# Rotary embedding and two pools' differences kept in their PSUM banks, in an encoder layer on one core

## The chip, the core and the metric

The kernel runs on one core of one Trainium2 chip. Five engines take part, each with its own in-order queue of instructions: TensorE (PE) multiplies matrices into the eight banks of PSUM, VectorE (DVE) and ScalarE (ACT) do element-wise work from and to SBUF and PSUM, GpSimd (POOL) does element-wise work in SBUF, and SyncE (SP) issues transfers. They wait for each other through semaphores. The metric is device time in microseconds, the median of three runs.

## What is computed

One layer of a bidirectional encoder, 512 tokens of width 1024: a half-step feed-forward block, a mixing block, another half-step feed-forward block and a final norm. The change touches the mixing block:

```python
u = rms_norm(h, mix_norm[l]) @ w_in[l]
q, k, v, pc = jnp.split(u, [512, 640, 768], axis=-1)
q = apply_partial_rope(q.reshape(B, S, 8, 64), cos, sin)     # first 16 of 64 dims
k = apply_partial_rope(k.reshape(B, S, 2, 64), cos, sin)
a = window_attention(q, k, v, sink_logits[l])                # 4 blocks of 128 tokens, +-128
# four groups of 128 channels, windows 2, 4, 8, 16:
p = ((mean_window(pc) - pc) @ pool_w) * pool_scale           # per group
h = h + concat([a, p]) @ w_out[l]
```

The rotation is `rot * cos + rot_half * sin`, where `rot_half` exchanges the two halves of the 16 rotated dimensions and negates one.

## The kernel before

Everything is kept transposed, channels on the 128 partitions and 512 tokens along the free dimension. Products are made to full precision out of three reduced-precision ones (`mm3`, L131 to L133): each operand is split into a high part, which ACT rounds (`wh`, `ah`, `pdh`, ...), and the rest, which DVE or POOL subtracts (`wl`, `al`, `pdl`, ...). Weights come in 1 MB transfers (`raw`) and are split half by half in `split_next` (L103, L104); a table says which halves of w_in and w_out POOL subtracts rather than DVE (`WIN_POOL`, `WOUT_POOL`, L30 and L32).

The mixing block (L356 on) runs so. PE projects keys and values, then pool group 3, query tile 0, pool group 2, query tiles 1, 2, 3, pool groups 1 and 0; each projection takes eight `mm3` and leaves its result in one PSUM bank. DVE rotates keys and queries in `rope` (L393): `stream_shuffle` from the bank into `rtmp`, bank times `cr` into `u`, `rtmp` times `sr` into `rtmp`, and the sum into `u`. ACT and DVE then split `u` into `kk`/`kl` (L419 to L421) or `qq` (L428, L429); two head halves of 64 partitions, a rounding by ACT and a subtraction by DVE for each. Values go through a transpose on PE and are split into `vv` and `vz` (L439 to L441); `vz` is a copy that DVE casts.

Each pool group starts in `pool_means` (L448): DVE scales the bank into `uu`; POOL widens the sums by doubling (`s`, L463), mends the edges (L469) and makes the sum `dd` (L472); DVE subtracts the token (`less_token`, L475); ACT and DVE split the difference into `pdh` and `pdl` (`halves`, L479, L480). These steps stand in lists (`later`) of which each step of the main flow takes one (`eased`), with `AFTER` empty steps ahead of the subtraction. `pool_linear` (L489) multiplies the difference by the group's matrix (the three matmuls ps<-pdh,pwh and so on), and first takes what is left of its list.

Attention goes by blocks of 128 tokens and two head groups of four: a score is two matmuls (L556, L557), a masked minimum on DVE (L558) and an exponential on ACT (L561); POOL scales the rows (L568); PE turns them (L585), ACT and DVE split them (`ph`, `pl`, L589, L590), and PE multiplies by the values (L600, L601). A plan (L656) weaves these with the last projections, the pool linears and the output projection. Ahead of the third and fourth score stand six fill matmuls each (L554). A scheduler places the instructions in each engine's queue and allots the banks; it may move an instruction forward or back among those of its engine, which the order below shows.

Of the kernel before, what the change touches and what calls it, by code (L numbers as in the profile page):

```python
# [8 lines left out]
F32 = mybir.dt.float32  # L9
F32R = mybir.dt.float32r  # L10
AF = mybir.ActivationFunctionType
ALU = mybir.AluOpType
# [3 lines left out]
S = 512  # L16
# [8 lines left out]
F0 = 3  # L25
WARM = 10
AFTER = 11
EARLY = 12
LAG = 4
WIN_POOL = (5,)  # L30
FIRST_SPARE = 7
WOUT_POOL = (0, 3, 6)  # L32
POOL_W = (2, 4, 8, 16)
PAD = 8

# [2 lines left out]
def encoder_layer(ctx: ExitStack, tc: tile.TileContext, xT, w1h, w1gu, w1d, win, wout, w2h, w2gu, w2d,  # L38
                  gains, gfin, sinks, poolw, pscale, cosT, sinT, edges, out):
    nc = tc.nc  # L40
# [112 lines left out]
    ps = bank()  # L153
# [202 lines left out]
    with tc.tile_pool(name="mix", bufs=1) as mp:  # L356
        cr = mp.tile([P, S], F32, name="cr")
        sr = mp.tile([P, S], F32, name="sr")
# [24 lines left out]
        vv = mp.tile([P, NT, 2, P], F32R, name="vv")  # L383
        vz = mp.tile([P, NT, 2, P], F32R, name="vz")
# [6 lines left out]
        swap = [i + 8 if i < 8 else i - 8 if i < 16 else i for i in range(32)]  # L391

        def rope(ps, rot):  # L393
            u = base.tile([P, S], F32, name="u", tag="u", bufs=2)
            nc.vector.stream_shuffle(rot, ps, swap)
            nc.vector.tensor_tensor(u, ps, cr, op=ALU.mult)
            nc.vector.tensor_tensor(rot, rot, sr, op=ALU.mult)
            nc.vector.tensor_tensor(u, u, rot, op=ALU.add)
            return u

        def project(box):

# [29 lines left out]
        def values():  # L432
            ps = bank()
            for b in range(NT):
                nc.tensor.transpose(ps[:, b * P:(b + 1) * P], vT[:, b * P:(b + 1) * P], ident)
            pv4 = ps.rearrange("p (b c) -> p b c", b=NT)
            for g in range(2):
                r, o = rows[g], rows[1 - g]
                nc.scalar.copy(vv[:, :, g, r], pv4[:, :, r])  # L439
                nc.vector.tensor_copy(vz[:, :, g, r], vv[:, :, g, r].bitcast(F32))  # L440
                nc.vector.tensor_tensor(vv[:, :, g, o], pv4[:, :, r], vv[:, :, g, r].bitcast(F32),  # L441
                                        op=ALU.subtract)

        pdh = mp.tile([P, 4, S], F32R, name="pdh")
        pdl = mp.tile([P, 4, S], F32R, name="pdl")
        later = []

        def pool_means(gi, ps):  # L448
            w = POOL_W[gi]
            half = w // 2  # L450
            e0 = 2 * (half - 1)
            uu = mp.tile([P, S + 128], F32, name="uu", tag="pl", bufs=3)[:, :S + 2 * PAD]
            n = S + 2 * PAD
            nc.gpsimd.memset(uu[:, :PAD], 0.0)
            nc.gpsimd.memset(uu[:, n - PAD:], 0.0)
            nc.vector.tensor_tensor(uu[:, PAD:PAD + S], ps, rstd, op=ALU.mult)
            box = {"cur": uu}

            def widen(step):
                m = n - 2 * step + 1  # L460
                cur = box["cur"]
                nxt = mp.tile([P, S + 128], F32, name="s1", tag="s1", bufs=2)
                nc.gpsimd.tensor_tensor(nxt[:, :m], cur[:, :m], cur[:, step:step + m], op=ALU.add)  # L463
                box["cur"] = nxt

            def scale():
                cur, o = box["cur"], PAD - half
                for a, e in ((o, e0), (o + S + 1 - half, e0 + half)):
                    nc.gpsimd.tensor_tensor(cur[:, a:a + half], cur[:, a:a + half], edge[:, e:e + half],  # L469
                                            op=ALU.mult)  # L470
                box["dd"] = mp.tile([P, S], F32, name="dd", tag="ph", bufs=3)
                nc.gpsimd.tensor_tensor(box["dd"], cur[:, o:o + S], cur[:, o + 1:o + 1 + S], op=ALU.add)  # L472

            def less_token():
                nc.vector.scalar_tensor_tensor(box["dd"], box["dd"], 0.5 / w, uu[:, PAD:PAD + S],  # L475
                                               op0=ALU.mult, op1=ALU.subtract)

            def halves():
                nc.scalar.copy(pdh[:, gi, :], box["dd"])  # L479
                nc.vector.tensor_tensor(pdl[:, gi, :], box["dd"], pdh[:, gi, :].bitcast(F32),  # L480
                                        op=ALU.subtract)

            wait = [lambda: None]
            steps = []
            while 1 << len(steps) < w:
                steps.append(lambda step=1 << len(steps): widen(step))
            later.append(steps + [scale] + (AFTER - len(steps)) * wait + [less_token, halves])

        def pool_linear(gi):  # L489
            while later[3 - gi]:  # L490
# [40 lines left out]
        last_pools = projected(1) + projected(0)  # L531
        weave([eased(f) for f in last_pools[:EARLY]], [])

# [208 lines left out]
def _arrange(inputs):  # L742
# [41 lines left out]
    rot = HD // 4  # L784
    inv = np.float32(500000.0) ** (-np.arange(0, rot, 2, dtype=np.float32) / np.float32(rot))
    ang = np.arange(S, dtype=np.float32)[None, :] * inv.astype(np.float32)[:, None]
    cosT = np.ones((P, S), np.float32)
    sinT = np.zeros((P, S), np.float32)
    for b in (0, HD):
        for j in range(rot // 2):  # L790
            cosT[b + j] = cosT[b + j + 8] = np.cos(ang[j])
            sinT[b + j] = -np.sin(ang[j])
            sinT[b + j + 8] = np.sin(ang[j])
    o["cosT"], o["sinT"] = cosT, sinT
    e = []
    for w in POOL_W:
# [28 lines left out]
```

## Time and profile before

| | us |
|---|---|
| median of 3 runs (lowest, highest) | 891.33 (891.25, 892.61) |
| the profiled execution | 892.52 |
| its span, first to last instruction | 890.7 |
| PE busy | 871.7 (98%) |
| DVE busy | 416.2 (47%) |
| ACT busy | 306.5 (34%) |
| POOL busy | 305.7 (34%) |
| mean granted clock of PE | 0.995 of full |

The shares are means over the whole span. The mixing block's first part, where projections end and attention starts, lies between about 385 and 465 us; the feed-forward blocks before and after it leave PE hardly any idle time. Matmul rows overlap, so PE counts as busy until the end of its last row, and a wait is printed in brackets behind the instruction that ended it, with the releasing engine, tile and line.

### The profile page before, as it was taken

The page shows a single profiled execution, that of the slowest core. Times are in us where ns is not written, and L with a number is a line of the kernel's source. Part 1 is how long each engine was busy: PE and PEld are TensorE (multiplying, and loading weights), DVE is VectorE, ACT ScalarE, POOL GpSimd, SP SyncE. Part 2 cuts the span into 40 slices and gives each one's busy share as a digit, 9 for nine tenths or more (in the row PEclk, how much of TensorE's full clock was granted, in tenths as well). Part 3 has the DMA queues.
Part 4 walks back from the last instruction along what each step waited for, and adds up shares of the span by engine and source line. Part 5 has one row for each costly group of instructions (what it writes and reads, how often), then busy time and mean ns, then how long its engine had stood idle before and what let it go on. Part 6 is the DMA issues. An engine that isn't in the chain of part 4 may idle for free.

```text
span 890.7 us, 9727 instructions
## 1 busy us (share of the span) xinstructions
PE 871.7 (98%) x3918; PEld 720.2 (81%) x3918; DVE 416.2 (47%) x519; ACT 306.5 (34%) x454; POOL 305.7 (34%) x252
## 2 busy tenths in 40 slices
PE   9999999999999999999689999999999999999996
PEld 7888888888888888888668888888888888888885
DVE  6454444444433322659788643444444444322235
ACT  7242222222223322623676532532222222222323
POOL 5085222222233330834452220762222322222214
PEclk9999999999999999999999999999999999999999
DMA  6412222222223322211111123122222222322302
GB/s 237 159 78 95 96 96 102 105 104 105 103 95 143 142 94 95 84 48 47 49 48 36 51 103 116 74 95 95 94 95 95 95 94 95 121 103 96 107 24 94
DMA packets 14683, 84.79 MB, mean 95 GB/s; under 512 B 1824, under 2 KB 2352, under 8 KB 5808
## 3 DMA queue, kind: packets, MB, share of 16 engines
q1 hardware_dynamic: 13104, 81.60, 25.6%
q10 hardware_dynamic: 1440, 2.57, 0.9%
q8 instruction: 30, 0.49, 0.2%
q14 instruction: 13, 0.11, 0.0%
q0 software_dynamic: 96, 0.02, 0.0%
HBM read 82.08 MB, written 2.10 MB: 95 GB/s over the span
## 4 chain that ended last, share of the span: by engine, by line
PE 92%; DVE 4%; POOL 2%; ACT 1%; issue 0%; DMA 0%; DVEq 0%; POOLq 0%
PE ps L131 29%; PE ps L133 29%; PE ps L132 29%; POOL s L463 1%; PE ps L585 1%; DVE qq L429 1%; PE ps L601 1%; PE ps L600 1%; DMA small<-in_gains 0%; DVE wl L104 0%; PE ps L556 0%; PE ps L694 0%; DVE pdl L480 0%; POOL dd L472 0%; PE ps L557 0%
## 5 line engine op out<-in xcount | busy, mean ns | idle before, releaser
L104 DVE TENSOR_TENSOR wl<-raw,wh 128x1024 fp32r<-128x1024 f32 (+2 forms) x145 | 218.5, 1510 | 193.9 <-ACT wh L103 191.5
L103 ACT CAST wh<-raw 128x1024 fp32r<-128x1024 f32 (+2 forms) x149 | 152.1, 1022 | 382.2 <-PE ps L132 336.0
L225 POOL TENSOR_TENSOR t<-t,t 128x512 f32<-128x512 f32 x44 | 76.8, 1750 | 212.7 <-ACT t L224 212.7
L131 PE MATMUL ps<-zh,wh 128*128 128x512 f32 x346 | 135.5, 392 | 0.0
L132 PE MATMUL ps<-zl,wh 128*128 128x512 f32 x346 | 135.1, 390 | 0.0
L133 PE MATMUL ps<-xh,wl 128*128 128x512 f32 x346 | 134.9, 390 | 0.0
L131 PE MATMUL ps<-xh,wh 128*128 128x512 f32 x346 | 134.9, 390 | 0.0
L133 PE MATMUL ps<-zh,wl 128*128 128x512 f32 x346 | 134.8, 390 | 0.0
L132 PE MATMUL ps<-xl,wh 128*128 128x512 f32 x346 | 134.6, 389 | 0.0
L273 POOL TENSOR_TENSOR al<-a,ah 128x512 fp32r<-128x512 f32 x44 | 66.4, 1512 | 127.8 <-ACT ah L272 127.8
L227 POOL TENSOR_TENSOR a<-t,rstd 128x512 f32<-128x512 f32 x44 | 62.1, 1415 | 99.4 <-DVE t L226 99.4
L226 DVE TENSOR_TENSOR t<-ps,t 128x512 f32<-128x512 f32 x44 | 30.4, 692 | 123.0 <-PE ps L133 108.3
L131 PEld LDWEIGHTS ps<-xh,wh 128*128 128x128 f32 x346 | 64.9, 188 | 13.9 <-ACT wh L103 0.3
L133 PEld LDWEIGHTS ps<-xh,wl 128*128 128x128 f32 x346 | 64.9, 188 | 14.0 <-issue 0.2
L133 PEld LDWEIGHTS ps<-zh,wl 128*128 128x128 f32 x346 | 64.9, 188 | 13.9 <-issue 0.2
L132 PEld LDWEIGHTS ps<-zl,wh 128*128 128x128 f32 x346 | 65.0, 188 | 13.6 <-issue 0.2
L132 PEld LDWEIGHTS ps<-xl,wh 128*128 128x128 f32 x346 | 64.9, 188 | 13.3
L131 PEld LDWEIGHTS ps<-zh,wh 128*128 128x128 f32 x346 | 65.0, 188 | 13.1
L223 DVE TENSOR_TENSOR t<-ps,rstd 128x512 f32<-128x512 f32 x44 | 30.2, 691 | 85.6 <-PE ps L133 77.3
L131 PE MATMUL ps<-ah,wh 128*128 128x512 f32 x176 | 68.5, 389 | 0.0
L132 PE MATMUL ps<-al,wh 128*128 128x512 f32 x176 | 68.5, 389 | 0.0
L133 PE MATMUL ps<-ah,wl 128*128 128x512 f32 x176 | 68.5, 389 | 0.0
(187 smaller groups left out, 1223.2 us busy)
## 6 DMA issues: line engine op xcount, KB each, us to landing
raw<-in_w1gu SPq DMA_DIRECT2D x19, 1024.0 KB, 4.7
raw<-in_w2gu SPq DMA_DIRECT2D x19, 1024.0 KB, 4.7
raw<-in_w1d SPq DMA_DIRECT2D x11, 1024.0 KB, 4.8
raw<-in_w2d SPq DMA_DIRECT2D x11, 1024.0 KB, 4.8
raw<-in_win SPq DMA_DIRECT2D x5, 1024.0 KB, 4.8
raw<-in_wout SPq DMA_DIRECT2D x4, 1024.0 KB, 4.8
raw<-in_w2h SPq DMA_DIRECT2D x4, 768.0 KB, 4.3
raw<-in_w1h SPq DMA_DIRECT2D x3, 768.0 KB, 4.5
```

Of the source, the lines that this page charges most:

```text
L103: nc.scalar.copy(wh[:, c:c + m], src[:, c:c + m])
L104: sub.tensor_tensor(wl[:, c:c + m], src[:, c:c + m], wh[:, c:c + m].bitcast(F32), op=ALU.subtract)
L131: nc.tensor.matmul(ps, lhsT=ah, rhs=bh, start=start, stop=False)
L132: nc.tensor.matmul(ps, lhsT=ah, rhs=bl, start=False, stop=False)
L133: nc.tensor.matmul(ps, lhsT=al, rhs=bh, start=False, stop=stop)
L223: nc.vector.tensor_tensor(t1, pg, rstd, op=ALU.mult)
L225: nc.gpsimd.tensor_tensor(t2, t2, t1, op=ALU.mult)
L226: nc.vector.tensor_tensor(t1, pu, t2, op=ALU.mult)
L227: nc.gpsimd.tensor_tensor(act[:, f, :], t1, rstd, op=ALU.mult)
L273: nc.gpsimd.tensor_tensor(al, act[:, k, :], ah.bitcast(F32), op=ALU.subtract)
L429: nc.vector.scalar_tensor_tensor(t[o, :], u[r, :], -HD ** -0.5, t[r, :].bitcast(F32), op0=ALU.mult, op1=ALU.subtract)
L463: nc.gpsimd.tensor_tensor(nxt[:, :m], cur[:, :m], cur[:, step:step + m], op=ALU.add)
```

## The change

Five edits. The rotation is reordered and works in the projection's own bank: bank times `sr` into `rtmp`, the shuffle from `rtmp` into `u`, bank times `cr` in place, the sum in place; the host's table `sinT` changes its signs for that. What splits keys and queries then reads the bank. The copy `vz` is made by ACT from PSUM rather than by DVE from SBUF. Pool groups 3 and 2 (`gi > 1`) put their difference into the projection's bank; groups 1 and 0 have 26 steps rather than 11 ahead of the subtraction, and their subtraction and second split are tied to the place in DVE's queue where the program has them (`keep_in_program_order`). POOL takes half 1 of w_out in place of half 3.

```diff
+LAST_AFTER = 26
-WOUT_POOL = (0, 3, 6)
+WOUT_POOL = (0, 1, 6)
...
         def rope(ps, rot):
             u = base.tile([P, S], F32, name="u", tag="u", bufs=2)
-            nc.vector.stream_shuffle(rot, ps, swap)
-            nc.vector.tensor_tensor(u, ps, cr, op=ALU.mult)
-            nc.vector.tensor_tensor(rot, rot, sr, op=ALU.mult)
-            nc.vector.tensor_tensor(u, u, rot, op=ALU.add)
-            return u
+            nc.vector.tensor_tensor(rot, ps, sr, op=ALU.mult)
+            nc.vector.stream_shuffle(u, rot, swap)
+            nc.vector.tensor_tensor(ps, ps, cr, op=ALU.mult)
+            nc.vector.tensor_tensor(ps, ps, u, op=ALU.add)
+            return ps
...
-                nc.vector.tensor_copy(vz[:, :, g, r], vv[:, :, g, r].bitcast(F32))
+                nc.scalar.copy(vz[:, :, g, r], pv4[:, :, r])
...
             def less_token():
-                nc.vector.scalar_tensor_tensor(box["dd"], box["dd"], 0.5 / w, uu[:, PAD:PAD + S],
-                                               op0=ALU.mult, op1=ALU.subtract)
+                dd = ps if gi > 1 else box["dd"]
+                keep(nc.vector.scalar_tensor_tensor(dd, box["dd"], 0.5 / w, uu[:, PAD:PAD + S],
+                                                    op0=ALU.mult, op1=ALU.subtract))
+                box["dd"] = dd
             def halves():
                 nc.scalar.copy(pdh[:, gi, :], box["dd"])
-                nc.vector.tensor_tensor(pdl[:, gi, :], box["dd"], pdh[:, gi, :].bitcast(F32),
-                                        op=ALU.subtract)
+                keep(nc.vector.tensor_tensor(pdl[:, gi, :], box["dd"], pdh[:, gi, :].bitcast(F32),
+                                             op=ALU.subtract))
+            def keep(ins):
+                if gi < 2:
+                    tc.keep_in_program_order(ins)
...
-            later.append(steps + [scale] + (AFTER - len(steps)) * wait + [less_token, halves])
+            later.append(steps + [scale] + ((AFTER if gi > 1 else LAST_AFTER) - len(steps)) * wait + [less_token, halves])
...
-            sinT[b + j] = -np.sin(ang[j])
-            sinT[b + j + 8] = np.sin(ang[j])
+            sinT[b + j] = np.sin(ang[j])
+            sinT[b + j + 8] = -np.sin(ang[j])
```

DVE's queue at the rotations of queries 2 and 3, before (ps_2754 is query 2's bank, ps_2795 query 3's):

```order
L395 STREAM_SHUFFLE rtmp_106<-ps_2754 128x512
L396 TENSOR_TENSOR u_2782<-ps_2754,cr_2463 128x512
L397 TENSOR_TENSOR rtmp_106<-rtmp_106,sr_2464 128x512
L398 TENSOR_TENSOR u_2782<-u_2782,rtmp_106 128x512
L429 SCALAR_TENSOR_TENSOR qq_2490<-u_2782,qq_2490 64x512 x2
L395 STREAM_SHUFFLE rtmp_106<-ps_2795 128x512
L396 TENSOR_TENSOR u_2820<-ps_2795,cr_2463 128x512
L397 TENSOR_TENSOR rtmp_106<-rtmp_106,sr_2464 128x512
L104 TENSOR_TENSOR wl_2867<-raw_2829,wh_2866 128x1024
L398 TENSOR_TENSOR u_2820<-u_2820,rtmp_106 128x512
L429 SCALAR_TENSOR_TENSOR qq_2490<-u_2820,qq_2490 64x512 x2
```

The same stretch of DVE's queue in the change, from query 2's sum on:

```order
L400 TENSOR_TENSOR ps_2754<-ps_2754,u_2782 128x512
L397 TENSOR_TENSOR rtmp_106<-ps_2795,sr_2464 128x512
L399 TENSOR_TENSOR ps_2795<-ps_2795,cr_2463 128x512
L431 SCALAR_TENSOR_TENSOR qq_2490<-ps_2754,qq_2490 64x512
L398 STREAM_SHUFFLE u_2820<-rtmp_106 128x512
L431 SCALAR_TENSOR_TENSOR qq_2490<-ps_2754,qq_2490 64x512
L400 TENSOR_TENSOR ps_2795<-ps_2795,u_2820 128x512
L431 SCALAR_TENSOR_TENSOR qq_2490<-ps_2795,qq_2490 64x512
L458 TENSOR_TENSOR uu_2860<-ps_2835,rstd_105 128x512
L105 TENSOR_TENSOR wl_3186<-raw_3183,wh_3185 128x1024
L431 SCALAR_TENSOR_TENSOR qq_2490<-ps_2795,qq_2490 64x512
```

Query 3's first operations stand ahead of query 2's splits, the two splits of a query stand apart, and the w_out half wl_2867 has left DVE.

DVE's queue where the scores begin, before (sc_2889 is block 0's first head group, dd_2881 pool group 1's difference):

```order
L558 ISA sc_2889,st_2890<-ps_2892,mask_2475,small_64 128x256
L558 ISA st_2890 128x1
L475 SCALAR_TENSOR_TENSOR dd_2881<-dd_2881,uu_2860 128x512
L558 ISA sc_2889,st_2890<-ps_2900,mask_2475,small_64 128x256
L558 ISA st_2890 128x1
```

DVE's queue in the change where that subtraction stands now (sc_2989 is block 1's second head group):

```order
L566 ISA sc_2989,st_2990<-ps_3025,mask_2475,small_64 128x384
L566 ISA st_2990 128x1
L478 SCALAR_TENSOR_TENSOR dd_2881<-dd_2881,uu_2860 128x512
L105 TENSOR_TENSOR wl_3324<-raw_3183,wh_3323 128x1024
L598 TENSOR_TENSOR pl_3037<-ps_3031,ph_3036 128x512
L484 TENSOR_TENSOR pdl_2548<-dd_2881,pdh_2547 128x512
```

Pool group 1's subtraction has moved from behind the first score to behind the sixteenth, and a w_out half that POOL had made follows it.

DVE's queue in the change at pool group 0's subtraction, dd_3013 (sc_3103 and sc_3137 are block 2's two head groups); before, it stands directly behind the sixteenth score, ahead of the first pl:

```order
L566 ISA sc_3103,st_3104<-ps_3132,mask_2475,small_64 128x384
L566 ISA st_3104 128x1
L566 ISA sc_3137,st_3138<-ps_3140,mask_2475,small_64 128x384
L566 ISA st_3138 128x1
L478 SCALAR_TENSOR_TENSOR dd_3013<-dd_3013,uu_3000 128x512
L574 RECIPROCAL st_3104<-st_3104 128x4
L484 TENSOR_TENSOR pdl_2548<-dd_3013,pdh_2547 128x512
```

PE's queue in the change at the same place, where ps_3148 is pool group 0's linear:

```order
L564 MATMUL ps_3140<-kk_2484,qq_2490 128x384
L565 MATMUL ps_3140<-kl_2485,qq_2490 128x384
L132 MATMUL ps_3148<-pdh_2547,pwh_2471 128x512
L133 MATMUL ps_3148<-pdl_2548,pwh_2471 128x512
L134 MATMUL ps_3148<-pdh_2547,pwl_2472 128x512
```

PE has the linear behind the same score as before; DVE's subtraction for it has moved from ahead of block 2's scores to behind the first one of its second head group.

## Rows read from the trace of the kernel before

**Rows 1.** Stretches: us; busy (count) of PE, PEld, DVE, ACT, POOL; PEclk; DMA share, GB/s.

```profile
425.91:438.38 12.47, 5.74 (x25) 4.76 (x24) 7.71 (x22) 6.60 (x14) 4.42 (x5) 0.86 0.22 85
...
444.73:452.03 7.30, 4.71 (x15) 3.41 (x14) 4.50 (x10) 4.96 (x12) 7.14 (x14) 0.77 0.41 144
452.03:464.00 11.97, 11.11 (x57) 7.97 (x57) 10.08 (x27) 9.69 (x26) 3.58 (x8) 1.00 0.01 1
...
434.96:438.38 3.42, 3.05 (x9) 2.77 (x10) 2.65 (x13) 2.42 (x8) 0.00 (x0) 0.50 0.01 2
```

**Rows 2.** Timeline of PE: start, duration, instruction, [idle before <-releaser].

```profile
413.78 0.39 PE L131 MATMUL ps<-yh,wh 128*128 128x512 f32 x1
...
421.94 0.28 PE L556 MATMUL ps<-kk,qq 128*128 128x256 f32 x1
...
424.68 1.50 PE L128 MATMUL ps<-ones 128*128 128x128 f32 x12
428.02 0.39 PE L556 MATMUL ps<-kk,qq 128*128 128x256 f32 x1 [1.84 <-DVE qq L429]
...
431.09 0.36 PE L556 MATMUL ps<-kk,qq 128*128 128x256 f32 x1 [1.13 <-DVE st L558]
...
435.33 0.69 PE L556 MATMUL ps<-kk,qq 128*128 128x384 f32 x1 [3.76 <-DVE st L558]
...
454.41 0.39 PE L131 MATMUL ps<-pdh,pwh 128*128 128x512 f32 x1
```

**Rows 3.** Timeline of DVE, 395 to 435 us.

```profile
395.41 2.16 DVE L420 TENSOR_TENSOR kl<-u,kk 64x512 fp32r<-64x512 f32 x2
397.60 0.69 DVE L396 TENSOR_TENSOR u<-ps,cr 128x512 f32<-128x512 f32 x1
...
402.88 2.91 DVE L429 SCALAR_TENSOR_TENSOR qq<-u,qq 64x512 fp32r<-64x512 f32 x2
405.81 1.05 DVE L440 CAST vz<-vv 128x256 fp32r<-128x256 f32 x1
...
412.72 1.22 DVE L104 TENSOR_TENSOR wl<-raw,wh 128x1024 fp32r<-128x1024 f32 x1
413.97 1.40 DVE L429 SCALAR_TENSOR_TENSOR qq<-u,qq 64x512 fp32r<-64x512 f32 x2
415.38 2.83 DVE L480 TENSOR_TENSOR pdl<-dd,pdh 128x512 fp32r<-128x512 f32 x1
...
422.80 0.73 DVE L395 STREAM_SHUFFLE rtmp<-ps 128x512 f32<-128x512 f32 x1
...
434.18 0.69 DVE L475 SCALAR_TENSOR_TENSOR dd<-dd,uu 128x512 f32<-128x512 f32 x1 [3.23 <-POOL dd L472]
```

**Rows 4.** Timeline of POOL in the same stretch.

```profile
395.51 4.68 POOL L463 TENSOR_TENSOR s<-s 128x525 f32<-128x525 f32 x3
...
403.86 2.86 POOL L463 TENSOR_TENSOR s<-s 128x525 f32<-128x525 f32 x2
...
415.29 2.39 POOL L104 TENSOR_TENSOR wl<-raw,wh 128x1024 fp32r<-128x1024 f32 x1 [6.51 <-ACT wh L103]
429.49 1.97 POOL L463 TENSOR_TENSOR s<-uu 128x527 f32<-128x527 f32 x1 [11.82 <-DVE uu L456]
```

**Rows 5.** Timeline of DVE at the scores and behind them, for spacings.

```profile
438.74 0.48 DVE L558 CUSTOM_DVE_ANT_0 sc<-ps,mask,small 128x256 f32<-128x256 f32 x1
...
439.15 0.62 DVE L558 CUSTOM_DVE_ANT_0 sc<-ps,mask,small 128x384 f32<-128x384 f32 x1
...
439.69 0.62 DVE L558 CUSTOM_DVE_ANT_0 sc<-ps,mask,small 128x384 f32<-128x384 f32 x1
...
448.62 0.74 DVE L496 SCALAR_TENSOR_TENSOR pdl<-ps,small,pdh 128x512 fp32r<-128x512 f32 x1
449.28 1.28 DVE L590 TENSOR_TENSOR pl<-ps,ph 128x512 fp32r<-128x512 f32 x2
```

**Rows 6.** Timeline of ACT: the cast of a pool's difference.

```profile
435.81 0.60 ACT L479 CAST pdh<-dd 128x512 fp32r<-128x512 f32 x1
```

## The prediction

> **What bounds the kernel now.** The page's busy shares (the table above) put TensorE (PE) at 98%, so time can be won only where PE waits or runs at its lower clock. I read the table of stretches next, for where that is: from 425.91 to 438.38 PE is busy 5.74 of 12.47 us, from 444.73 to 452.03 4.71 of 7.30, and from there to 464.00 it is idle for 0.86 [rows 1]. That is the attention's start, which is the place of the edit. PE's rows name what ended each wait: 1.84 us for the queries' low halves (qq, L429), 1.13 and 3.76 us for score reductions (L558) [rows 2]. All three are VectorE (DVE). Its rows show why it is late. The same operation takes very different times: two qq operations take 2.91 us and later 1.40, pdl takes 2.83 us, where a 512-wide operation costs 0.69 [rows 3]. Beside the long ones GpSimd (POOL) runs s (403.86 for 2.86 us) and wl (415.29 for 2.39 us) [rows 4]. All the long ones read two tensors from SBUF, or are a cast within SBUF (vz, 1.05). An operation that reads one operand from PSUM (u<-ps,cr at 397.60) takes 0.69 us in the middle of POOL's additions of 395.51 to 400.19 [rows 3, 4]. Then DVE stands 3.23 us at 434.18 for POOL's sum, dd, with finished scores queued behind it [rows 3].
>
> **Part 1, rotations and pools 3 and 2 in PSUM, vz on ScalarE.** Query 3's projection is done at 413.78, where PE goes on to the next one [rows 2]; DVE only starts its rotation at 422.80 [rows 3], so it is 9.0 us behind. What leaves the queue before it: the qq pair of 402.88 falls from 2.91 to 1.40 (1.5), pdl of 415.38 from 2.83 to 0.69 (2.1), the kl pair from 2.16 to two spacings of 0.60 and a tail of 0.09, 1.3 (0.9), the cast of 1.05 goes to ScalarE, and query 2's qq pair (1.4) now stands behind query 3's first operations. Together 6.9. Against that the first rotation begins after cr and sr rather than before: 0.6. So query 3's rotation starts 0 (the smaller collisions, not counted here, are gone too) to 2.7 us after its projection, at 413.8 to 416.5. Its last qq comes ten operations later: rtmp, ps, two qq of query 2, shuffle, add, qq, uu, wl (1.13 net of the overlap, from 1.22 [rows 3]), qq, about 7.6 us with one wait for ScalarE, so at 421.4 to 424.1. The fourth score, the first that needs query 3, stands behind a group of fill matmuls that ends no earlier than 426.0 (424.68 and 1.3 of its 1.50) [rows 2]. The queries are then early by 2 us or more, and the 1.84 goes.
>
> ScalarE and DVE now alternate on a query's bank (half, half, half, half) where ScalarE formerly ran ahead; that adds one ScalarE pass, 0.6, per query, covered by the same 2 us. No row shows a DVE operation that writes PSUM. Lower end: no dearer than one that reads it, 0.69 as in SBUF; a gain is not excluded, but DVE would only wait for PE sooner, so it is worth nothing. Upper end: twice, 0.6 more for each of ten writes before the last qq and two subtractions. I take the lower, since the nearest row (397.60) shows no surcharge at that port. [...]
>
> The in-place operations' freedom from POOL is read from 397.60 alone. [...]
>
> **Part 2, pool 1's subtraction moved behind sixteen scores.** At 434.18 DVE no longer waits for POOL in front of the scores, so the 3.76 and the 1.13 go. [...] In this stretch PE so gets back 6.7 of waits and 1.7 of clock, 8.4.
>
> **Part 3, the price: pool 0's subtraction, tied.** PE's order is nearly the same, and after the first score of block 2's second head group stands pool 0's linear (L131, ps<-pdh,pwh), which started at 454.41 [rows 2]. It needs pdh of pool 0, hence the tied subtraction, which DVE now reaches after that very score. So this point is set by DVE's queue. Count from the fourth score, 426.0 plus 0.4 for its two matmuls, 426.4. Until the subtraction there are 5 scores of 256 at 0.41 (438.74 to 439.15), 13 of 384 at 0.54 (439.15 to 439.69), ten plain 512-wide operations (four pl, two sums, uu, pool 1's dd and pdl, qq) at 0.60 (the pl pair of 1.28), three pdl of the linears at 0.66 (448.62 to 449.28) [rows 5], one wl at 1.13 and four reciprocals at 0.1: 2.0 + 7.0 + 6.0 + 2.0 + 1.1 + 0.4 = 18.5. To it come collisions with POOL, which scales sc at the time, for the three with two SBUF inputs (dd, wl, pdl), and short waits for ScalarE's exponentials and PE's products. Lower end 0; upper end 4.5, by 0.8 for each collision (as the qq pair, 1.5 for two) and 2 of waits. I take 2.4, in the middle, since both kinds occur in [rows 3]. So the subtraction starts at 447.3 (444.9 to 449.4), takes 0.69, the cast pdh 0.60 [rows 6] and handing over 0.1: PE starts the linear at 448.7 (446.3 to 450.8) in place of 454.41. That is **5.7 us earlier (3.6 to 8.1)**.
>
> PE itself would be there at 421.94 + 32.5 less 8.4 and less the 4.3 lost from 444.73 to 452.03 (2.6 idle, and 1.7 of clock, granted at 0.77 on the mean [rows 1]), 441.7, plus 1 to 3 of new waits for pl behind the moved dd and wl: it stands 4 to 6 us, so a new wait takes the place of half of the old ones. Behind it PE loses another 1.7 to the clock, as after 3.76 before, and about 0.6 for pdl; before it still lost 0.9 idle from 452.03 to 464.00 [rows 1] and about 1 in lengthened steps. I set these against each other at nothing, with 0.8 either way.
>
> **Part 4, the rest at nothing.** The w_out half that changes place costs POOL 2.39 at a time when it has nothing (it idles between 417.7 and 429.5 [rows 4]), and takes 1.13 from DVE before the queries and puts it behind the scores, where it is counted. vz on ScalarE is two short casts while that engine mostly waits for DVE. The other table's signs are made on the host. SP's transfers keep their order.
>
> **The sum.** The profiled execution took 892.52 us with a span of 890.7; less 5.7 that is 886.8 and 885.0. The median of the three runs is 1.2 below the profiled one; from it the forecast is 891.33 - 5.7 = **885.6 us**, with an own range of 883.0 to 888.0.
>
> **Rivals.**
> - *The pool-0 wait is short.* DVE meets no POOL work after the scores: 18.5 in place of 20.9, and PE's clock stays up. Gain 8.1 to 9: 882.8. For it: POOL finishes its scaling earlier too. Against: it scales two more blocks in just this time.
> - *It gives all back.* Collisions and waits at their upper end (4.5), the second clock drop counted in full and the new waits for pl lowering the clock once more (1.7): 5.7 - 2.1 - 1.7 = 1.9 or less, 889.4 or more: at the edge of what a measurement of this kernel can tell from no change (0.2%, about 1.8 us).
> - *Writing PSUM is dear, and it is slower.* At 0.6 more per write, twelve writes cost 7.2, of which 2 to 3 are covered: 1 us of gain is left, 890.3. From about 0.7 on nothing is left; at 1.2 (three times the price) 14.4 less 2.5 is 11.9, and 891.33 - 5.7 + 11.9 = 897.5. For it: no row. Against: reads at 0.69.
> - *It doesn't do what it says: operations with a PSUM operand still wait for POOL.* Then part 1 gives 2.4 in place of 6.9, the queries are late by some 2 to 3 us, and part 3's chain starts 2 to 4 later and is longer by 2 to 3 more collisions: between 886 and 893. Against it the row at 397.60.
>
> **How the numbers follow.** Forecast 0.70; short wait 0.12; all given back 0.08; dear writes 0.05; collisions stay 0.05. The range runs from the short wait, 882.8, to 889.2, just under the third case; it leaves out the last three for the most part and the short wait's lower end, 0.19. Faster by over 0.2% (below 889.5): the first two, 0.82, and half of the third, 0.86. Same: the other half and a part of the fourth and fifth, 0.07. Slower (above 893.1): the rest of these two, 0.07.
>
> **What would show it.** Right: no wait of PE over 1 us between 421.9 and about 432; qq at 0.69 throughout; one wait of 4 to 6 us before pool 0's linear, named by pdh of ScalarE, at about 443 to 449, with the clock at 0.50 behind it; the last qq before 424; DVE busy almost without gaps from 426 to 447. Wrong: shuffles or writes into ps longer than 0.75, PE waits for qq, or a linear that starts after 452.

## The result and the profile after

The changed kernel takes **886.68 us** (median of four runs, 886.52 to 887.15); the kernel before, run beside it, 891.97 (four runs, 891.25 to 892.76). The ratio is 0.9941, with a 95% interval of 0.9924 to 0.9959: faster by 0.6%. The profiled execution of the change took 886.76 us with a span of 884.8, against 892.52 and 890.7.

Where the 5.9 us of span went can be read from two points of PE's queue, the first score and pool 0's linear. Before, they start at 421.94 and 454.41 [rows 2], 32.47 us apart. PE's rows after (start, duration, instruction, wait and its releaser; rows left out are a score's second matmul and the scores between):

```profile
422.18 0.28 PE L564 MATMUL ps<-kk,qq 128*128 128x256 f32 x1
...
424.92 1.50 PE L129 MATMUL ps<-ones 128*128 128x128 f32 x12
426.18 0.36 PE L564 MATMUL ps<-kk,qq 128*128 128x256 f32 x1
...
438.34 0.51 PE L608 MATMUL ps<-ph,vv 128*128 128x512 f32 x1 [0.17 <-ACT ph L597]
439.40 0.50 PE L608 MATMUL ps<-ph,vv 128*128 128x512 f32 x1 [0.56 <-ACT ph L597]
...
442.95 0.34 PE L565 MATMUL ps<-kl,qq 128*128 128x384 f32 x1
448.87 0.79 PE L132 MATMUL ps<-pdh,pwh 128*128 128x512 f32 x1 [5.58 <-ACT pdh L483]
449.77 0.79 PE L133 MATMUL ps<-pdl,pwh 128*128 128x512 f32 x1
```

They are now 26.69 us apart, 5.78 less. From the linear to the end it is 884.8 - 448.87 = 435.93 against 436.29, and the first score comes 0.24 later; 5.78 + 0.36 - 0.24 is the whole difference. The fourth score follows its fill matmuls without a wait, and no score behind it has one; the waits of 1.84, 1.13 and 3.76 us [rows 2] are gone. Two more waits have shrunk, those at the first products with the values, now 0.17 and 0.56 us (438.34 and 439.40). PE's rows of the kernel before have there:

```profile
446.42 0.50 PE L600 MATMUL ps<-ph,vv 128*128 128x512 f32 x1 [1.21 <-ACT ph L589]
...
448.76 0.80 PE L601 MATMUL ps<-pl,vz 128*128 128x512 f32 x1 [1.38 <-DVE pl L590]
```

These five were 9.3 us together; in the change there are 0.7 us of them, and one new wait of 5.58 us at pool 0's linear. The stretches of the change follow (columns as in [rows 1]: PE, PEld, DVE, ACT and POOL busy with their counts, PEclk, DMA share, GB/s).

```profile
421.90:436.00 14.10, 14.10 (x100) 13.28 (x100) 10.78 (x39) 11.52 (x34) 10.14 (x18) 1.00 0.01 2
436.00:440.00 4.00, 3.12 (x12) 1.58 (x11) 4.00 (x6) 3.51 (x7) 3.76 (x6) 1.00 0.42 131
442.95:448.87 5.92, 0.34 (x2) 0.01 (x1) 5.19 (x15) 4.62 (x13) 2.94 (x5) 0.71 0.00 0
445.39:452.21 6.82, 3.23 (x8) 2.53 (x9) 4.27 (x12) 3.62 (x10) 5.36 (x8) 0.50 0.00 0
452.21:464.00 11.79, 11.79 (x69) 9.91 (x68) 9.52 (x24) 8.44 (x20) 2.65 (x6) 1.00 0.01 2
```

PE is busy throughout the first 14 us, where before it was busy 5.74 of the 12.47 us from 425.91 [rows 1]. From 442.95 it has 0.34 us of work in 5.92, and from 445.39 to 452.21 its clock is granted at 0.50. It is one such stretch, of 6.82 us; before, there was one of 3.42 us and a second within 444.73 to 452.03, where the mean was 0.77 [rows 1]. DVE's rows at the rotations, in the change:

```profile
395.04 0.70 DVE L400 TENSOR_TENSOR ps<-ps,u 128x512 f32<-128x512 f32 x1
...
396.23 0.70 DVE L399 TENSOR_TENSOR ps<-ps,cr 128x512 f32<-128x512 f32 x1
396.83 0.68 DVE L422 TENSOR_TENSOR kl<-ps,kk 64x512 fp32r<-64x512 f32 x1
...
400.65 0.68 DVE L431 SCALAR_TENSOR_TENSOR qq<-ps,qq 64x512 fp32r<-64x512 f32 x1
401.26 0.90 DVE L478 SCALAR_TENSOR_TENSOR ps<-dd,uu 128x512 f32<-128x512 f32 x1
...
403.37 0.69 DVE L484 TENSOR_TENSOR pdl<-ps,pdh 128x512 fp32r<-128x512 f32 x1
...
414.23 0.68 DVE L397 TENSOR_TENSOR rtmp<-ps,sr 128x512 f32<-128x512 f32 x1
...
420.66 1.22 DVE L105 TENSOR_TENSOR wl<-raw,wh 128x1024 fp32r<-128x1024 f32 x1
421.90 0.69 DVE L431 SCALAR_TENSOR_TENSOR qq<-ps,qq 64x512 fp32r<-64x512 f32 x1
```

The same kl and qq that took 2.16 and 2.91 us as pairs [rows 3], where an unhindered pair takes 1.40 (413.97 [rows 3]), take 0.68 and 0.69 each, and they do so beside POOL's additions (POOL's rows):

```profile
393.92 3.59 POOL L465 TENSOR_TENSOR s<-s 128x525 f32<-128x525 f32 x3
...
400.54 2.53 POOL L465 TENSOR_TENSOR s<-s 128x525 f32<-128x525 f32 x2
...
420.82 1.98 POOL L465 TENSOR_TENSOR s<-uu 128x527 f32<-128x527 f32 x1 [3.24 <-DVE uu L458]
...
424.44 1.04 POOL L474 TENSOR_TENSOR dd<-s 128x512 f32<-128x512 f32 x1
```

The three additions now take 3.59 instead of 4.68 us [rows 4], so POOL lost time to the collisions too. Query 3's rotation starts at 414.23 instead of 422.80. Of these 8.6 us the three long rows of [rows 3], against 1.40 for a pair and 0.69 for pdl, make 4.4 (0.8 for kl, 1.5 for qq, 2.1 for pdl). The two last rows answer to the one at 429.49 with 11.82 idle [rows 4]: pool 1's sum starts 8.7 us earlier and is ready at 425.5. The experiments show that this matters.

### The profile page after: what moved, and what is told of

Its sections match the earlier page's. It is cut to its first block, busy times and chain, and to the rows that moved or that the text cites. A ratio compares the mean times of both kernels' runs of the same rounds, so it can differ in the third digit from the quotient of the medians.

```text
span 884.8 us, 9724 instructions
## 1 busy us (share of the span) xinstructions
PE 869.1 (98%) x3918; PEld 719.2 (81%) x3918; DVE 412.7 (47%) x517; ACT 308.0 (35%) x456; POOL 303.8 (34%) x252
## 4 chain that ended last, share of the span: by engine, by line
PE 97%; ACT 1%; DVE 1%; DMA 1%; issue 0%; DVEq 0%; ACTq 0%; POOLq 0%
PE ps L134 31%; PE ps L133 31%; PE ps L132 31%; PE ps L593 1%; ACT sc L569 1%; PE ps L608 1%; DMA small<-in_gains 1%; PE ps L609 1%; PE ps L564 0%; PE ps L565 0%; PE ps L702 0%; PE ps L239 0%; PE ps L241 0%; PE ps L243 0%; PE ps L129 0%; PE ps L216 0%
```

## The experiments

The theory in short: DVE was late because what read two SBUF tensors lost time to POOL (pdl 2.83 us against 0.69, a qq pair 2.91 against 1.40); the operands in PSUM take that away (0.68 to 0.69 each), and this is the gain. The late, tied subtraction of pool 0 is the price, since DVE's in-order queue then keeps PE's linear waiting (5.58 us). The rivals: that the moved subtractions gave the gain, or the new order of the rotation, or vz and w_out's half.

The table gives the ratio to the kernel before, run beside each on the same chip, and from each profile the first score's start, the time from there to pool 0's linear, the linear's wait, and the time from the first score to the span's end. The last column leaves out what comes before the attention, where profiles of unlike kernels differ by up to 1.8 us without a pattern (first score at 421.69 to 423.52).

| kernel | us | ratio (95%) | first score | to pool 0's linear | its wait | to the end |
|---|---|---|---|---|---|---|
| before | 891.97 | 1 | 421.94 | 32.47 | none | 468.8 |
| the change | 886.68 | 0.9941 (0.9924, 0.9959) | 422.18 | 26.69 | 5.58 | 462.6 |
| part1_alone | 883.17 | 0.9902 (0.9889, 0.9915) | 423.52 | 22.86 | none | 459.2 |
| part2_alone | 896.29 | 1.0048 (1.0035, 1.0060) | 422.01 | 36.11 | 5.16 | 472.6 |
| sbuf_results | 895.45 | 1.0037 (1.0024, 1.0050) | 423.32 | 35.15 | 5.59 | 472.2 |
| rotation_sbuf | 893.81 | 1.0007 (0.9998, 1.0016) | 421.93 | 33.74 | 5.58 | 470.8 |
| pools_sbuf | 887.90 | 0.9942 (0.9930, 0.9955) | 421.69 | 27.24 | 5.58 | 463.2 |
| old_rotation_order | 889.70 | 0.9963 (0.9949, 0.9976) | 422.13 | 27.62 | 5.58 | 464.4 |
| vz_and_wout_back | 887.12 | 0.9936 (0.9923, 0.9948) | 422.03 | 26.58 | 5.77 | 463.4 |
| untied | 887.77 | 0.9945 (0.9930, 0.9960) | 422.11 | 22.91 | none | 463.7 |
| early_pool0 | 881.59 | 0.9885 (0.9872, 0.9898) | 423.31 | 21.37 | 0.22 | 457.7 |
| early_pools | 881.77 | 0.9877 (0.9864, 0.9891) | 422.17 | 21.40 | none | 457.7 |
| both_early | 882.36 | 0.9886 (0.9871, 0.9901) | 421.76 | 22.24 | 1.28 | 458.1 |

Beside the experiments the kernel before had medians of 892.7 to 893.1, so ratios are compared below rather than times.

**Each half alone: part1_alone and part2_alone.** The first is the kernel before with the rotations, pools 3 and 2 and vz as in the change. Against the change it differs by this:

```diff
-LAST_AFTER = 26
...
-WOUT_POOL = (0, 1, 6)
+WOUT_POOL = (0, 3, 6)
...
-                if gi < 2:
-                    tc.keep_in_program_order(ins)
+                return ins
...
-            later.append(steps + [scale] + ((AFTER if gi > 1 else LAST_AFTER) - len(steps)) * wait + [less_token, halves])
+            later.append(steps + [scale] + (AFTER - len(steps)) * wait + [less_token, halves])
```

The second has these lines as in the change, and rotations (with their table's signs), pools 3 and 2 and vz as before:

```diff
-            nc.vector.tensor_tensor(rot, ps, sr, op=ALU.mult)
-            nc.vector.stream_shuffle(u, rot, swap)
-            nc.vector.tensor_tensor(ps, ps, cr, op=ALU.mult)
-            nc.vector.tensor_tensor(ps, ps, u, op=ALU.add)
-            return ps
+            nc.vector.stream_shuffle(rot, ps, swap)
+            nc.vector.tensor_tensor(u, ps, cr, op=ALU.mult)
+            nc.vector.tensor_tensor(rot, rot, sr, op=ALU.mult)
+            nc.vector.tensor_tensor(u, u, rot, op=ALU.add)
+            return u
...
-                nc.scalar.copy(vz[:, :, g, r], pv4[:, :, r])
+                nc.vector.tensor_copy(vz[:, :, g, r], vv[:, :, g, r].bitcast(F32))
...
-                dd = ps if gi > 1 else box["dd"]
+                dd = box["dd"]
```

> The kernel before with rotations and the first two pools' differences in PSUM and vz on ScalarE; the last two pools and w_out's halves stay as they were before. Theory (collisions with POOL made the queries late, and a late subtraction is only worth something while POOL's sum is late): query 3's rotation starts near 414 instead of 422.80, the 1.84 us wait for qq is gone, and because pool 1's sum is then ready at about 425.5 (POOL's row of the change, 424.44 and 1.04) DVE hardly stands for it either, so the 3.76 goes too although the subtraction is not moved; pool 0's linear does not wait 5.58 us. So it is as fast as the whole change or up to 4 us faster: 882.5 to 886.7, I take 884. Rival (the moved subtractions gave the gain, as my sum had it for 3.76 and 1.13): DVE still stands about 3 us behind the first scores, and the kernel stays at 889 to 891.

> The kernel before with only the last two pools' subtractions late and tied and with w_out's other half on POOL; rotations and the first two pools stay in SBUF, vz on DVE. Theory: qq pairs of 2.91 us and the pdl of 2.83 us stay, so the 1.84 us wait stays; the 3.76 wait goes from the first scores, but DVE reaches pool 0's tied subtraction some 6 us later than in the change, at about 453, so PE's linear starts near 454.5 as before (454.41) behind a wait of 5 to 6 us: 890.5 to 893.5, no gain. Rival (the moved subtractions gave the gain): 886 to 888. Rival (each half gave half): 889.

Part 1 alone is faster than the whole change (0.9902 against 0.9941, intervals apart), and part 2 alone is slower than the kernel before. That is plainer than the theory had it: the late subtractions do not only give nothing, they cost 0.4 to 0.5% with the new rotations and without them. DVE's rows of part1_alone say why pool 1's subtraction need not be moved:

```profile
423.97 0.69 DVE L430 SCALAR_TENSOR_TENSOR qq<-ps,qq 64x512 fp32r<-64x512 f32 x1
424.70 0.48 DVE L564 CUSTOM_DVE_ANT_0 sc<-ps,mask,small 128x256 f32<-128x256 f32 x1
...
426.43 0.69 DVE L477 SCALAR_TENSOR_TENSOR dd<-dd,uu 128x512 f32<-128x512 f32 x1 [1.24 <-POOL dd L473]
427.04 0.48 DVE L564 CUSTOM_DVE_ANT_0 sc<-ps,mask,small 128x256 f32<-128x256 f32 x1
```

DVE waits for the sum 1.24 us instead of 3.23 [rows 3], and this in front of scores whose fill matmuls PE is still doing: PE's first wait of this stretch comes at 438.34 (0.22 us). It is not without loss: DVE stands 2.67 us at 439.21 for pool 0's sum, and the low halves behind it come late for PE, whose 128x512 matmuls then start 0.43 us apart (442.56 to 443.84) against 0.23 at 428.08; 0.43 is also their spacing in the change where the clock is granted at 0.50 (450.36 to 450.79). PE's row:

```profile
440.62 0.64 PE L607 MATMUL ps<-pl,vz 128*128 128x512 f32 x1 [1.55 <-DVE pl L596]
```

In part2_alone the old chain is there in full, and the new wait behind it. PE's rows:

```profile
428.38 0.44 PE L563 MATMUL ps<-kk,qq 128*128 128x256 f32 x1 [2.12 <-DVE qq L430]
...
435.40 0.44 PE L563 MATMUL ps<-kk,qq 128*128 128x384 f32 x1 [1.12 <-DVE st L565]
...
458.12 0.80 PE L132 MATMUL ps<-pdh,pwh 128*128 128x512 f32 x1 [5.16 <-ACT pdh L482]
```

I had put this linear at 454.5; it came at 458.12, and the loss I did not expect is that. The 3.76 us wait has shrunk to 1.12, but DVE carries its lateness on into block 2.

**The place of the operands: sbuf_results, rotation_sbuf and pools_sbuf.** The change with results back in SBUF, the new order kept; in the first both edits, in the second only the rotation's, in the third only the pools':

```diff
-            nc.vector.tensor_tensor(ps, ps, cr, op=ALU.mult)
-            nc.vector.tensor_tensor(ps, ps, u, op=ALU.add)
-            return ps
+            nc.vector.tensor_tensor(rot, ps, cr, op=ALU.mult)
+            nc.vector.tensor_tensor(u, rot, u, op=ALU.add)
+            return u
...
-                dd = ps if gi > 1 else box["dd"]
+                dd = box["dd"]
```

> The changed kernel with its reordered rotation, its vz on ScalarE and its late pools, but with the rotation's products and sum and the first two pools' differences in SBUF tiles. Theory (the place of the operands is what counts, not the order of the operations): qq pairs take 2.8 us or more beside POOL's sums again, a wait of 1.5 to 2 us for qq returns ahead of the fourth score, pool 0's linear starts at 453 to 455: 890.5 to 894. Rival (the order of the rotation, vz and the late pools gave the gain): within 1 us of the change, 886 to 888.

> The changed kernel with only the rotation's product with cr and its sum back in SBUF tiles; the first two pools' differences stay in PSUM, the late pools as in the change. Theory (the qq and kl pairs and the rotation's sums, which read two SBUF tensors again, make the lateness; five rotations, about 1.5 us each for the pair and some for the sum): the wait for qq ahead of the fourth score returns (1.5 to 2 us), pool 0's linear starts at 452 to 454 instead of 448.87: 890 to 894. Rival (the pools' place counts as much as the rotations'): half of the loss, 888 to 889.5.

> The changed kernel with only the first two pools' differences back in SBUF (their subtraction and second split read two SBUF tensors again); the rotations stay in PSUM. Theory: up to four operations can collide with POOL, at most 2.1 us as the pdl of 2.83 did before, but in the change the last qq ends at about 422.6 and the fourth score follows its fill matmuls at 426.18, so there are 3.6 us of slack: nothing lost, 886 to 887.5. By my prediction's sum pdl carries 2.1 of the 6.9 us that the lateness loses; if that lateness still counted, it would be 888.5 to 889.

All three came out on the theory's side, though not in every figure: rotation_sbuf's wait for qq is 0.58 us instead of 1.5 to 2, and its linear comes at 455.67 instead of 452 to 454. With the rotation's results in SBUF the whole gain is gone (1.0007). With both edits undone it is worse than the kernel before (1.0037), by more than I expected, since the linear comes at 458.47 and not at 453 to 455: the late pools cost more on a late queue, as in part2_alone. Not all of rotation_sbuf's loss is collisions. The scheduler also drew another order for DVE, in which it stands for pool 3's sum early on, as it does in sbuf_results (2.74 us) and not in the change:

```profile
399.40 0.70 DVE L478 SCALAR_TENSOR_TENSOR ps<-dd,uu 128x512 f32<-128x512 f32 x1 [2.73 <-POOL dd L474]
```

How the loss divides between this stand and the lengthened operations was not tried; in the kernel before that stand was 0.88 us (402.16). Three of DVE's rows of rotation_sbuf show the collision in one place, with POOL's row beside them:

```profile
422.18 0.75 DVE L398 STREAM_SHUFFLE u<-rtmp 128x512 f32<-128x512 f32 x1
422.97 0.69 DVE L399 TENSOR_TENSOR rtmp<-ps,cr 128x512 f32<-128x512 f32 x1
423.69 1.63 DVE L400 TENSOR_TENSOR u<-rtmp,u 128x512 f32<-128x512 f32 x1
```

```profile
422.39 2.38 POOL L105 TENSOR_TENSOR wl<-raw,wh 128x1024 fp32r<-128x1024 f32 x1 [5.97 <-PE ps L565]
```

The shuffle (one SBUF input) and the product with one PSUM input run at their normal 0.75 and 0.69 in the middle of POOL's wl. The sum of two SBUF tensors, which starts at 423.69, ends at 425.32, 0.55 us after wl does (422.39 + 2.38 = 424.77). With the pools' differences in SBUF the time is that of the change, although the collision is there. DVE and POOL in pools_sbuf:

```profile
409.63 2.75 DVE L484 TENSOR_TENSOR pdl<-dd,pdh 128x512 fp32r<-128x512 f32 x1
...
423.30 0.69 DVE L431 SCALAR_TENSOR_TENSOR qq<-ps,qq 64x512 fp32r<-64x512 f32 x1
```

```profile
409.43 2.40 POOL L105 TENSOR_TENSOR wl<-raw,wh 128x1024 fp32r<-128x1024 f32 x1 [4.71 <-ACT wh L104]
```

Here pdl again ends 0.55 us after wl (412.38 against 411.83). The last qq comes 1.4 us later than in the change, within what PE's fill matmuls cover. So the pools' half of part 1 is not needed once the rotations are in PSUM. With the rotations in SBUF it is: sbuf_results and rotation_sbuf differ in it alone, and 1.0037 against 1.0007 is 0.3%, intervals apart.

**The order of the rotation: old_rotation_order.** The change with the old four operations and the old signs, the products and the sum in the bank:

```diff
-            nc.vector.tensor_tensor(rot, ps, sr, op=ALU.mult)
-            nc.vector.stream_shuffle(u, rot, swap)
+            nc.vector.stream_shuffle(rot, ps, swap)
             nc.vector.tensor_tensor(ps, ps, cr, op=ALU.mult)
-            nc.vector.tensor_tensor(ps, ps, u, op=ALU.add)
+            nc.vector.tensor_tensor(rot, rot, sr, op=ALU.mult)
+            nc.vector.tensor_tensor(ps, ps, rot, op=ALU.add)
```

> The changed kernel with the rotation's old order (shuffle out of the bank into rtmp, bank times cr in place, rtmp times sr within SBUF, sum in place) and the old signs of the table. Theory: only rtmp times sr reads two SBUF tensors now, one possible collision of 0.3 to 1.5 us per rotation; the 3.6 us of slack ahead of the fourth score take that up: 886 to 888. Rival (the new order carries the gain, since each rotation loses 1.5 or more): 889 to 892.

The expectation was missed: 889.70 us is in the rival's range, and 0.9963 of the 891.97 beside the change is 888.7, between the two and outside the theory's 886 to 888. The intervals of 0.9963 and of the change's 0.9941 overlap; the profiled span is 1.7 us longer. The fourth score still does not wait, so the slack was there. Collisions do not explain it: the one I spoke of shows once, 1.12 us at 419.03, while DVE stands 1.84 us at 401.50 for pool 3's sum, which it does not in the change. But the last qq and uu come 2.2 us later, and DVE's queue behind the scores with them. Its rows there:

```profile
422.25 0.69 DVE L456 TENSOR_TENSOR uu<-ps,rstd 128x512 f32<-128x512 f32 x1
...
424.11 0.69 DVE L429 SCALAR_TENSOR_TENSOR qq<-ps,qq 64x512 fp32r<-64x512 f32 x1
...
435.53 1.23 DVE L476 SCALAR_TENSOR_TENSOR dd<-dd,uu 128x512 f32<-128x512 f32 x1
```

Pool 1's subtraction starts at 435.53 instead of 434.76, and pool 0's linear at 449.75 instead of 448.87. That is 0.9 of the 1.7. The rest goes with the clock, which was granted at 0.87 from 452 to 464 us where the change has 0.99. In pools_sbuf uu and qq were late too, by 1.4 us each (421.44 and 423.30), and it cost nothing that can be measured. Which of the two makes the difference was not tried.

**vz and the w_out half: vz_and_wout_back.**

```diff
-WOUT_POOL = (0, 1, 6)
+WOUT_POOL = (0, 3, 6)
...
-                nc.scalar.copy(vz[:, :, g, r], pv4[:, :, r])
+                nc.vector.tensor_copy(vz[:, :, g, r], vv[:, :, g, r].bitcast(F32))
```

> The changed kernel with the cast of vz back on DVE (from SBUF, within SBUF) and half 3 instead of half 1 of w_out on POOL. Theory (part 4 of the prediction: worth nothing, since the slack of 3.6 us ahead of the fourth score takes up a cast of 0.3 to 1.05 us, and POOL has nothing else at the time): 886 to 887.5. Rival (vz on DVE collides with POOL's sums twice, 1 us each, and w_out's half meets the sums of the last pools): 888 to 890.

Nothing, as expected: 0.9936 against 0.9941.

**The price: untied, early_pool0, early_pools, both_early.** The first takes the two ties away:

```diff
-                if gi < 2:
-                    tc.keep_in_program_order(ins)
+                return ins
```

The other three keep them and change how many empty steps stand ahead of pool 0's and pool 1's subtraction: 8 and 26 in early_pool0 (shown), 8 and 22 in early_pools, 8 and 11 in both_early.

```diff
-LAST_AFTER = 26
+LAST_AFTER = (8, 26)
...
-            later.append(steps + [scale] + ((AFTER if gi > 1 else LAST_AFTER) - len(steps)) * wait + [less_token, halves])
+            later.append(steps + [scale] + ((AFTER if gi > 1 else LAST_AFTER[gi]) - len(steps)) * wait + [less_token, halves])
```

> The changed kernel without the ties (26 empty steps stay, but the scheduler may move the last two pools' subtraction and split forward in DVE's queue). It does so with both subtractions (pool 1's to ahead of the first score, pool 0's to behind the sixteenth) and leaves pool 0's second split, pdl, behind the scores of block 2. Theory (PE's wait is set by the last of the chain subtraction, pdh, pdl in the in-order queues): DVE stands about 2 to 3 us for POOL's sum ahead of the first score, and PE loses 1 us or more there or behind; PE no longer waits for pdh at pool 0's linear but for pdl, 2 to 3 us at its second matmul: 885 to 888, about the change. Rival (the place of the subtraction alone sets the 5.58): 881 to 882.5, as with the early pool 0.

> The changed kernel with 8 instead of 26 empty steps ahead of pool 0's subtraction alone; it is still tied and now stands behind the third pl, at about 441, and no longer behind the first score of block 2's second group; POOL's sum for it was ready at 435.3. Theory (the 5.58 us that PE stands ahead of pool 0's linear are the price of the late place, and its clock drop with them): that wait is gone, some 1 to 1.5 us come back as short waits for pl and scores, which are delayed by the 0.9 and 0.9 of the subtraction and the second split: 881 to 883.5, 3 to 6 us better than the change. Rival (DVE is simply full there, and whatever stands ahead of the linear waits as long): the wait turns up at the value products or the scores, 885 to 888.

> The changed kernel with 8 empty steps ahead of pool 0's subtraction and 22 ahead of pool 1's, instead of 26 for both; pool 1's subtraction so stands behind uu of pool 0 (433.1 in the run with pool 0 alone moved) and three scores earlier than there. Theory: the first pl no longer stands behind a subtraction of 1.12, a wl of 1.21 and the short waits for ph of 0.18 and 0.56 and PE's lost time around 438 to 440 (1.6 us altogether) shrink: 880 to 881.5 against 881.6. Rival (DVE's queue has the same work either way): 881.6 within 0.7.

> The changed kernel with 8 empty steps ahead of pool 0's subtraction and 11 ahead of pool 1's, both still tied; pool 1's now stands behind the sixth score. Theory (with the queries early, pool 1's sum is ready at about 425.5, before DVE gets there, so its late place is worth nothing any more): as with pool 0 alone early, ratio to the kernel before 0.987 to 0.990, about 881 to 883 in the run with a kernel before of 892. Rival (my prediction's step that the moved subtraction gives back 3.76 and 1.13 of waits and 1.7 of clock): DVE stands again in the scores, 885 or more.

Moving pool 0's subtraction alone takes the wait away (0.22 us for 5.58) and with it the clock's fall (1.00 from 440 to 452.21, where the change has 0.50 from 445.39). Rows of DVE, of PE and of the stretch around, in early_pool0:

```profile
441.40 0.68 DVE L478 SCALAR_TENSOR_TENSOR dd<-dd,uu 128x512 f32<-128x512 f32 x1
...
443.26 0.68 DVE L484 TENSOR_TENSOR pdl<-dd,pdh 128x512 fp32r<-128x512 f32 x1
```

```profile
444.68 0.47 PE L132 MATMUL ps<-pdh,pwh 128*128 128x512 f32 x1 [0.22 <-DVE rtmp L614]
...
447.86 0.63 PE L593 MATMUL ps<-ident,sc 128*128 128x128 f32 x4 [0.61 <-DVE st L574]
```

```profile
440.00:452.21 12.21, 10.80 (x53) 7.87 (x54) 12.15 (x31) 9.70 (x24) 4.80 (x12) 1.00 0.18 75
```

The ratio is 0.9885: 0.6% better than the change. The wait did not come back elsewhere (0.61 us is the longest up to 460), although DVE is busy 12.15 of 12.21 us. Where pool 1's subtraction stands then makes no difference: with 26, 22 and 11 steps the ratios are 0.9885, 0.9877 and 0.9886. The small gain that I expected of 22 is not there. From the first score to the end these three take 457.7 to 458.1 us against part1_alone's 459.2, whose wait of 1.55 us they do not have and whose mean granted clock of 0.995 is lower than theirs (0.998 and 0.999); by the ratios they can't be told from it for certain (0.9902, intervals overlapping).

Without the ties the subtraction goes forward but the second split stays behind the scores, so PE waits at the linear's second matmul instead of its first (PE's rows of untied):

```profile
450.12 0.79 PE L133 MATMUL ps<-pdl,pwh 128*128 128x512 f32 x1 [2.38 <-DVE pdl L484]
...
452.11 0.80 PE L132 MATMUL ps<-pdh,wh 128*128 128x512 f32 x1 [0.78 <-ACT pdh L502]
```

The time is that of the change. Pool 1's subtraction also went forward here, ahead of the first score, where DVE stands 2.91 us for POOL's sum (425.44); PE loses 0.47 us to that at a score. The tie is not what costs, and an early subtraction alone is not what helps: both the subtraction and pdl have to stand ahead of the scores. The three kernels with pool 0's subtraction early (early_pool0, early_pools, both_early) beat both the kernel before and the change, and can't be told apart.

## Why the prediction was right, and where it was not

- **The time.** Forecast 885.6, measured 886.68, inside the range and inside the forecast's own 883.0 to 888.0. The sum was one term, pool 0's linear 5.7 us earlier; that point moved 5.78 measured from the first score, and 5.54 on the clock of the traces (454.41 to 448.87).
- **Part 1.** Query 3's rotation starts at 414.23 (forecast 413.8 to 416.5), the last qq at 421.90 and ends at 422.6 (421.4 to 424.1), the fourth score at 426.18 (426.0); there is no wait for qq. Writes into PSUM take 0.69 to 0.70 (0.90 for the one from two SBUF tensors at 401.26), so the lower end was right and the rival of dear writes falls. What I read from 397.60 alone, that an operation with one operand in PSUM loses nothing to POOL, shows again in rotation_sbuf: beside POOL's wl the product with a PSUM input took 0.69, the sum of two SBUF tensors 1.63.
- **A term of part 1 that bought nothing here.** I counted pdl's 2.1 us among the 6.9. The saving is real (2.83 to 0.69), but pools_sbuf shows that with the rotations in PSUM the time does not depend on it. I had listed the slack of 2 us or more in the same paragraph and did not set the term against it.
- **Part 2 is the step that failed.** I credited the moved subtraction of pool 1 with 3.76 and 1.13 of waits and 1.7 of clock (my estimate: half of the 3.42 us from 434.96 to 438.38, granted at 0.50 [rows 1]). In part1_alone these waits and these slow matmuls are gone although nothing is moved there (PE is busy for the whole of 426 to 438, and its 128x512 matmuls at 428.08 start 0.23 us apart, where those of the kernel before start 0.43 apart from 436.13 to 436.99), and both_early keeps pool 1's 11 steps at the best time. What I missed stands in [rows 4]: POOL idled 11.82 us for uu. uu stood in DVE's queue behind the late rotations, so part 1 already brings pool 1's sum forward, to 425.5. I followed DVE's lateness to PE but not to POOL and back.
- **Part 3.** Subtraction forecast at 447.3, measured 447.26; linear 448.7, measured 448.87; wait 4 to 6, measured 5.58. DVE's queue was nearly gapless (19.51 us busy of the 20.86 from 426.40 to 447.26), with just the operations that I had counted. Of the 2.4 us for collisions and waits the collisions were the smaller part: the subtraction of pool 1 and its pdl lost 0.7 together, wl none (435.80, 1.21), and most of the rest was waits. That the middle of a range of 4.5 us held to 0.1 (447.26 less 426.4 and 18.5 is 2.36) was luck:

```profile
434.76 1.11 DVE L478 SCALAR_TENSOR_TENSOR dd<-dd,uu 128x512 f32<-128x512 f32 x1
...
437.54 0.95 DVE L484 TENSOR_TENSOR pdl<-dd,pdh 128x512 fp32r<-128x512 f32 x1
...
447.26 0.91 DVE L478 SCALAR_TENSOR_TENSOR dd<-dd,uu 128x512 f32<-128x512 f32 x1
...
448.85 0.86 DVE L484 TENSOR_TENSOR pdl<-dd,pdh 128x512 fp32r<-128x512 f32 x1 [0.60 <-ACT pdh L483]
```

- **What the price was.** I took the late pools for the price of a gain that they do not make. By the experiments part 1 alone is worth 0.98% (9.6 us from the first score to the end), and the late pools take 0.39% of it back. The forecast held all the same, because its sum was the linear's new time, counted along DVE's queue from the fourth score, and part 2's 8.4 us do not enter that count.
- **Part 4 and the rivals.** Part 4 is worth nothing, as forecast. The wait at pool 0's linear was not short (5.58), operations that read a PSUM operand did not wait for POOL (0.68 at 400.65, beside its additions), and the balance behind the linear was close to nothing (0.36 us gained from there to the end), so the gain was not given back.

## What to carry to other kernels

When GpSimd works beside VectorE, look for VectorE operations that read two SBUF tensors and give one of them a PSUM home (here pdl fell from 2.83 to 0.69 us); do it first for what stands on the path to the next matmul, since time saved where there is slack buys nothing (pools_sbuf). When a queue is relieved, follow what it feeds on every engine before moving anything else: a wait may already be gone. An operation that is put off in an in-order queue must come, with all that its consumer needs, ahead of the point where that consumer is next in TensorE's own order (TensorE waited 5.58 us in the change, 2.38 in untied, 0.22 in early_pool0); part1_alone and early_pool0 show that a good change can hide a costly one.

## What was not expected of the hardware

- Three operations with two SBUF inputs that ran beside GpSimd's wl ended just behind it: two 0.55 us after it (425.32 against 424.77, 412.38 against 411.83), and pdl of the kernel before 0.53 after (418.21 against 417.68 [rows 3, 4]). The largest losses of a single operation that are shown here, 2.1 us each (pdl at 2.83 and 2.75 against 0.69), were beside a wl of 2.4 us.
- The result's place does not help by itself: the subtraction of two SBUF tensors into PSUM at 401.26 took 0.90 beside POOL's additions, where the kind takes 0.69.
- GpSimd loses as well: the same three additions took 4.68 and 3.59 us with and without the collisions, and pool 1's first addition, started 0.16 us behind DVE's wl, took 1.98 (420.82) where pool 0's took 1.07 (432.73).
- A cast within SBUF, with one SBUF input, lost time too: vz took 1.05 us beside GpSimd's additions (405.81 [rows 3]) and 0.29 behind them (400.66).
